# A row-maximum kernel: the last three rows in four pieces of three quarters of a row, with other sizes of loads and shares

## Chip, cores, metric

One NeuronCore of a Trainium2 chip. The metric is the device time of one execution in microseconds (us). A program on one core is timed in several runs. The profiled span is 1.8 us shorter than the time (162.3 of 164.08 us in the profiled run before).

## The reference

```python
x = np.random.randn(32, 512, 1024).astype(np.float32)
def reference(x):
    return np.max(x, axis=-1).astype(np.float32)     # 32 x 512 maxima
```

67.1 MB have to be read, and 16384 rows of 1024 numbers reduced. Each of the 128 partitions holds 128 rows.

## The kernel before

Rows come in loads of falling size into a ring of 46 row places. VectorE takes each row's maximum with a free-axis reduction. It is slightly too slow to reach the end with the loads (an estimate from the trace: at the 1.042 ns an element worked out in the prediction, the 83 rows left at 74.64 us would take it 88.6 us, to 163.2, and the last piece lands at 159.0), so some rows' first columns are shared: TensorE *turns* blocks of 128 columns (transposes them into PSUM), ScalarE copies them to SBUF, GpSimd takes the maximum over partitions, TensorE *sends back* the maxima (one transpose of a 1x128 line per block) into a small PSUM tile `fetched`. VectorE writes its own part of the same rows into one further column of that tile, and later *merges* the tile's columns into the result.

```python
BLOCKS = [
    [15, 15, 15, 14, 12, 11, 9, 8, 7, 6],        # rows a load, numbered 0 to 9
    [4, 3, 2, 2, 1, 1, 1],                       # loads 10 to 16; then two rows more
]
RING = 46
SHARED = {7: (2, 3), 9: (4, 4), 11: (3, 3), 13: (2, 3), 16: (1, 1)}   # load: (rows, blocks of 128 columns)
TENSOR = [                                       # TensorE's order: what, load, chunk
    ("turn", 7, 0), ("back", 7, 0), ("turn", 9, 0), ("turn", 9, 1),
    ("back", 9, 0), ("turn", 11, 0), ("turn", 11, 1), ("back", 9, 1),
    ...
]
MERGE = {8: (7,), 12: (9,), 15: (11,), 18: (13, 16)}   # after the work of load 8 merge load 7, ...
# ... (cut) ...
for j in range(len(loads)):
    # ... (cut: issue loads up to three ahead, then TensorE's orders that are due) ...
    if n > m:
        maximum(res[:, col:col + n - m], rows(j)[:, :n - m, :])          # own rows
    if m and parts < C:
        maximum(share(j)[:, parts, :], rows(j)[:, n - m:, parts * P:])   # own part of shared rows
    merge(j)
# the last two rows, as pieces of 689, 671 and 688 columns
piece = ring[:, at, :D - K]
nc.sync.dma_start(out=piece, in_=xb[:, S - 2, :D - K])
pair = xb[:, S - 2:, :].rearrange("p i d -> p (i d)")
nc.sync.dma_start(out=res[:, AT:AT + K + W], in_=pair[:, D - K:D + W])
nc.sync.dma_start(out=res[:, MID:], in_=pair[:, D + W:])
latest_row = maximum(res[:, AT - 1:AT], piece)
# ... (cut: the middle piece's two halves in one reduction, the merges) ...
maximum(res[:, I - 1:I], res[:, MID - 1:])
```

## Time and profile before

| | before |
|---|---|
| time, median (runs of the prediction) | 164.06 us |
| VectorE busy | 135.4 us |
| mean of the DMA over the span | 414 GB/s |
| last piece lands / last reduction ends | 159.0 / 160.0 us |
| GpSimd's last work ends | 158.3 us |

Lines of the timeline: start (us), length (us), engine, line, operation, out<-in, shapes, count.

```profile
149.72 1.01 PE L161 MATMUL fetched<-ident,top 1*128 1x1 f32 x8
...
152.42 0.17 DVE L168 TENSOR_REDUCE res<-fetched 128x4 f32<-128x20 f32 x1
```

The reader is to see a distance: the 6-row load's maxima are sent back by 150.73 (149.72 + 1.01), and VectorE merges them at 152.42. The merge has 1.7 us to spare, because it is asked for after load 12 only.

### The profile page before, as it was taken

Reading aid. Unit: us, or ns where it says so; the run is one execution under the profiler, and the core shown is the slowest. Engines: PE = TensorE matmul, PEld = TensorE weight load, DVE = VectorE, ACT = ScalarE, POOL = GpSimd, SP = SyncE. Lnnn points to the kernel's source line nnn. Section 1 sums busy time; section 2 is a strip of 40 time slices with the busy share of each in tenths; the row PEclk is TensorE's granted clock in tenths of the full one; section 3 lists DMA queues with packets and bytes.
Section 4 is the critical chain, followed back from the end, with each engine's and each line's share of the span. In section 5 each row is a group of like instructions: output and inputs, shape, how many; then the busy total and the mean of one; then the engine's idle time right before and its main releaser. Section 6 shows DMA issues by size and latency. Waiting matters only on the chain.

```text
span 162.3 us, 305 instructions
## 1 busy us (share of the span) xinstructions
PE 14.0 (9%) x76; PEld 12.0 (7%) x76; DVE 135.4 (83%) x35; ACT 6.3 (4%) x8; POOL 16.2 (10%) x11
## 2 busy tenths in 40 slices
PE   0000000000000000000000000000003010736540
PEld 0000000000000000000000000000002010725440
DVE  3000079995999779998999999999999999999994
ACT  3000000000000000000000000000001000222020
POOL 0000000000000000000000000000000500095970
DMA  7999699988999699999998998999999999999990
GB/s 242 485 485 454 273 485 485 485 379 348 485 485 485 285 410 452 452 452 388 497 472 371 433 455 355 436 436 420 509 396 445 452 395 396 440 411 423 405 379 18
DMA packets 3200, 67.18 MB, mean 414 GB/s; under 512 B 640, under 2 KB 640, under 8 KB 1408
## 3 DMA queue, kind: packets, MB, share of 16 engines
q1 hardware_dynamic: 2880, 67.11, 96.7%
q10 hardware_dynamic: 320, 0.07, 0.2%
HBM read 67.11 MB, written 0.07 MB: 414 GB/s over the span
## 4 chain that ended last, share of the span: by engine, by line
DVE 57%; DMA 36%; issue 5%; DVEq 0%
DVE res L168 52%; DMA ring<-in_x_dram 36%; DVE fetched L168 5%; DVEq L249 0%
## 5 line engine op out<-in xcount | busy, mean ns | idle before, releaser
L168 DVE TENSOR_REDUCE res<-ring 128x15 f32<-128x15360 f32 (+10 forms) x15 | 124.1, 8302 | 23.7 <-DMA ring<-in_x_dram 23.7
L143 POOL PARTITION_ALL_REDUCE top<-sb x7 | 16.0, 2330 | 141.8 <-ACT sb L141 141.8
L135 PE MATMUL ps<-ident,ring 128*128 128x128 f32 x38 | 9.3, 425 | 133.8 <-DMA ring<-in_x_dram 133.8
L135 PEld LDWEIGHTS ps<-ident,ring 128*128 128x128 f32 x38 | 7.5, 223 | 134.1 <-issue 127.8
L141 ACT COPY sb<-ps 128x768 f32<-128x768 f32 (+3 forms) x7 | 5.1, 739 | 150.2 <-PE ps L135 150.2
L168 DVE TENSOR_REDUCE fetched<-ring 128x2 f32<-128x1280 f32 (+3 forms) x5 | 8.5, 1699 | 0.0
L161 PE MATMUL fetched<-ident,top 1*128 1x1 f32 x38 | 4.8, 243 | 10.8 <-DVE fetched L168 7.3
L161 PEld LDWEIGHTS fetched<-ident,top 1*128 1x128 f32 x38 | 4.5, 213 | 12.5 <-issue 8.0
L168 DVE TENSOR_REDUCE res<-res 128x2 f32<-128x672 f32 (+1 forms) x2 | 1.7, 858 | 0.0
L141 ACT ACT_TABLE_LOAD x1 | 1.3, 1283 | 0.7 <-PEq L238 0.7
L83 DVE MEMSET ident<- 128x128 f32 x1 | 0.2, 165 | 0.8 <-PEq L238 0.8
L168 DVE TENSOR_REDUCE res<-fetched 128x2 f32<-128x8 f32 (+3 forms) x5 | 0.7, 158 | 0.0
L90 DVE TENSOR_SCALAR rowno<-rowno 32x1 f32<-32x1 f32 x3 | 0.4, 146 | 0.1
L85 DVE TENSOR_TENSOR_SCAN colno<-ident 128x128 f32<-128x128 f32 x1 | 0.4, 425 | 0.0
L92 DVE TENSOR_SCALAR ident<-colno,rowno 128x128 f32<-128x128 f32 x1 | 0.3, 285 | 0.0
L87 DVE STREAM_TRANSPOSE rowno<-colno 128x32 f32<-128x32 f32 x1 | 0.2, 213 | 0.0
L238 POOL MEMSET const-float32-0.0<- 128x1 f32 x1 | 0.1, 98 | 0.2 <-issue 0.2
L238 POOL MEMSET const-bfloat16-1.0<- 128x1 bf16 x1 | 0.1, 101 | 0.0
L238 POOL MEMSET const-uint8-127<- 128x1 uint8 x1 | 0.1, 101 | 0.0
L238 POOL MEMSET const-float32-1.0<- 128x1 f32 x1 | 0.1, 99 | 0.0
L84 DVE MEMSET rowno<- 128x32 f32 x1 | 0.1, 85 | 0.0
## 6 DMA issues: line engine op xcount, KB each, us to landing
ring<-in_x_dram SPq DMA_DIRECT2D x3, 7680.0 KB, 38.4
ring<-in_x_dram SPq DMA_DIRECT2D x1, 7168.0 KB, 37.0
ring<-in_x_dram SPq DMA_DIRECT2D x1, 6144.0 KB, 33.4
ring<-in_x_dram SPq DMA_DIRECT2D x1, 5632.0 KB, 28.6
ring<-in_x_dram SPq DMA_DIRECT2D x1, 4608.0 KB, 39.1
ring<-in_x_dram SPq DMA_DIRECT2D x1, 4096.0 KB, 33.3
ring<-in_x_dram SPq DMA_DIRECT2D x1, 3584.0 KB, 29.0
ring<-in_x_dram SPq DMA_DIRECT2D x1, 3072.0 KB, 35.9
```

The lines of the kernel that those rows point to most:

```text
L83: in_turn("DVE", nc.vector.memset(ident, 1.0))
L84: in_turn("DVE", nc.vector.memset(rowno, 0.0))
L85: in_turn("DVE", nc.vector.tensor_tensor_scan(out=colno, data0=ident, data1=ident, initial=-1.0, op0=ALU.add, op1=ALU.mult))
L87: in_turn("DVE", nc.vector.transpose(out=rowno, in_=colno[:, :32]))
L90: in_turn("DVE", nc.vector.tensor_scalar(out=part, in0=part, scalar1=float(q * 32), scalar2=None, op0=ALU.add))
L92: in_turn("DVE", nc.vector.tensor_scalar(out=ident, in0=colno, scalar1=rowno[:, 0:1], scalar2=None, op0=ALU.is_equal))
L135: in_turn("PE", nc.tensor.transpose(out=ps[:, k * P:(k + 1) * P], in_=rows(j)[:, loads[j][1] - m + r + i, c0 * P:(c0 + 1) * P], identity=i ...
L141: in_turn("ACT", nc.scalar.copy(out=sb[:, :W], in_=ps[:, :W]))
L143: in_turn("POOL", nc.gpsimd.partition_all_reduce(top[:, :W], sb[:, :W], P, bass_isa.ReduceOp.max))
L161: in_turn("PE", nc.tensor.transpose(out=share(j)[:, c0, r + i:r + i + 1], in_=tops[j, c][0:1, k * P:(k + 1) * P], identity=ident[0:1, 0:1],))
L168: return in_turn("DVE", nc.vector.reduce_max(out=out, in_=in_, axis=X))
L238: nc = _bacc.Bacc("TRN2", target_bir_lowering=False, num_devices=1)
```

## The change

Intent: the last three rows come in four pieces of three quarters of a row; VectorE takes maxima of quarters, which one more instruction merges; GpSimd ends sooner, for the latest shared row falls away. To fit, the sizes of the loads and the shares are drawn anew. The core of the diff:

```diff
-    [15, 15, 15, 14, 12, 11, 9, 8, 7, 6],
-    [4, 3, 2, 2, 1, 1, 1],
+    [15, 15, 15, 14, 11, 10, 9, 9, 8, 6],
+    [4, 3, 2, 2, 1, 1],
-SHARED = {7: (2, 3), 9: (4, 4), 11: (3, 3), 13: (2, 3), 16: (1, 1)}
+SHARED = {8: (3, 3), 9: (5, 2), 10: (3, 3), 11: (2, 3), 13: (2, 3)}
 TENSOR = [
-    ("turn", 7, 0), ("back", 7, 0), ("turn", 9, 0), ("turn", 9, 1),
-    ("back", 9, 0), ("turn", 11, 0), ("turn", 11, 1), ("back", 9, 1),
-    ("turn", 13, 0), ("back", 11, 0), ("back", 11, 1), ("turn", 16, 0),
-    ("back", 13, 0), ("back", 16, 0),
+    ("turn", 8, 0), ("turn", 8, 1), ("back", 8, 0), ("back", 8, 1),
+    ("turn", 9, 0), ("turn", 9, 1), ("turn", 10, 0), ("turn", 10, 1),
+    ("back", 9, 0), ("back", 9, 1), ("turn", 11, 0), ("back", 10, 0),
+    ("back", 10, 1), ("turn", 13, 0), ("back", 11, 0), ("back", 13, 0),
 ]
-MERGE = {8: (7,), 12: (9,), 15: (11,), 18: (13, 16)}
+MERGE = {9: (8,), 10: (9,), 12: (10,), 14: (11,), 18: (13,)}
 # ... (the three pieces of before are removed) ...
+    last = xb[:, S - 3:, :].rearrange("p i d -> p (i d)")
+    for t in range(3):
         # ... (cut: place in the ring) ...
+        nc.sync.dma_start(out=piece, in_=last[:, t * 3 * Q:(t + 1) * 3 * Q])      # Q = 256
+        inst = maximum(tail[:, 7 + 3 * t:10 + 3 * t], piece.rearrange("p (q d) -> p q d", d=Q))
         # ... (cut: the stores' dependence on the second piece) ...
+        merge(len(loads) + t)
+    nc.sync.dma_start(out=tail[:, 16:], in_=last[:, 9 * Q:])
+    maximum(res[:, I - 3:I - 1], tail[:, 7:15].rearrange("p (r q) -> p r q", q=4))
+    maximum(res[:, I - 1:], tail[:, 15:])
```

More of the change, by code (lines that the diff above doesn't have):

```diff
@@ L59 @@
     ring = once.tile([P, RING, D], F32)
-    W = 336
-    K = W - 1
-    AT = I + 16
-    MID = AT + K + W + 17
-    res = once.tile([P, MID + D - W], F32)
+    res = once.tile([P, I], F32)
+    Q = D // 4
+    tail = once.tile([P, 16 + 3 * Q], F32)
     latest = {}
@@ L98 @@
     for sizes in BLOCKS:
-        S = sum(sizes) + 2 * (sizes is BLOCKS[-1])
+        S = sum(sizes) + 3 * (sizes is BLOCKS[-1])
         xb = xf[first * P:(first + S) * P, :].rearrange("(p i) d -> p i d", p=P)
@@ L199 @@
         back(i, c)
-    if at + 1 > RING:
-        at = 0
-    piece = ring[:, at, :D - K]
-    nc.sync.dma_start(out=piece, in_=xb[:, S - 2, :D - K])
-    pair = xb[:, S - 2:, :].rearrange("p i d -> p (i d)")
-    nc.sync.dma_start(out=res[:, AT:AT + K + W], in_=pair[:, D - K:D + W])
-    nc.sync.dma_start(out=res[:, MID:], in_=pair[:, D + W:])
-    latest_row = maximum(res[:, AT - 1:AT], piece)
-    merge(len(loads))
-    maximum(
-        bass.AP(tensor=res.tensor, offset=res.offset + I - 2,
-                ap=[list(res.ap[0]), [MID - 1 - (I - 2), 2]]),
-        res[:, AT - 1:AT + K + W].rearrange("p (r k) -> p r k", r=2))
-    merge(len(loads) + 1)
-    maximum(res[:, I - 1:I], res[:, MID - 1:])
+    last = xb[:, S - 3:, :].rearrange("p i d -> p (i d)")
+    for t in range(3):
+        if at + 1 > RING:
+            at = 0
+        piece = ring[:, at, :3 * Q]
+        at += 1
+        nc.sync.dma_start(out=piece, in_=last[:, t * 3 * Q:(t + 1) * 3 * Q])
+        inst = maximum(tail[:, 7 + 3 * t:10 + 3 * t], piece.rearrange("p (q d) -> p q d", d=Q))
+        if t == 1:
+            latest_row = inst
+        merge(len(loads) + t)
+    nc.sync.dma_start(out=tail[:, 16:], in_=last[:, 9 * Q:])
+    maximum(res[:, I - 3:I - 1], tail[:, 7:15].rearrange("p (r q) -> p r q", q=4))
+    maximum(res[:, I - 1:], tail[:, 15:])
     for p, q in ((0, 48), (48, 96), (96, P)):
```

## The prediction

A wait of about 0.5 us makes 164.55 (from 164.06), no wait 164.1, weighed about 3 to 1 that is 164.45 us.

> **What bounds the kernel now.** I read the page's tenths first, then the chain of waits, then the DMA issues together with the times of issue, and last the timeline of the final 35 us.
>
> The tenths (40 slices of the span) and the DMA's busy share:
>
> ```profile
> PE   0000000000000000000000000000003010736540
> DVE  3000079995999779998999999999999999999994
> POOL 0000000000000000000000000000000500095970
> DMA  7999699988999699999998998999999999999990
> ```
>
> Two rows are full at once. The DMA is full from the first slice to the last but one; VectorE idles only in the first half and is full afterwards. GpSimd and TensorE work only in the last quarter, where they take some columns off VectorE's hands. The chain of waits says which of the two full rows ended last:
>
> ```profile
> DVE 57%; DMA 36%; issue 5%; DVEq 0%
> ```
>
> In order of time (start, us) that chain leaves the DMA at 74.6 us and never comes back to it:
>
> ```profile
> 37.60 37.02 DMA ring<-in_x_dram
> 74.62 0.02 issue
> 74.64 55.86 DVE res L168 x5
> 130.50 1.40 DVE fetched L168
> ```
>
> But VectorE is only just not waiting. Landings follow from the DMA issues (last column: us from issue to landing) plus the time of issue. The last four rows of the page's kind, and the issue times in the timeline:
>
> ```profile
> ring<-in_x_dram SPq DMA_DIRECT2D x1, 344.5 KB, 18.3
> res<-in_x_dram SPq DMA_DIRECT2D x1, 344.0 KB, 11.5
> res<-in_x_dram SPq DMA_DIRECT2D x1, 335.5 KB, 14.3
> ```
>
> ```profile
> 138.93 0.33 SPq L204 DMA_DIRECT2D ring<-in_x_dram  x1
> 143.82 0.33 SPq L206 DMA_DIRECT2D res<-in_x_dram  x1
> 147.52 0.33 SPq L207 DMA_DIRECT2D res<-in_x_dram  x1
> ```
>
> So the last three pieces land at 157.2, 158.1 and 159.0 us, and VectorE takes them up at 157.34, 158.24 and 159.15:
>
> ```profile
> 157.34 0.86 DVE L168 TENSOR_REDUCE res<-ring 128x1 f32<-128x689 f32 x1
> 158.24 0.85 DVE L168 TENSOR_REDUCE res<-res 128x2 f32<-128x672 f32 x1
> 159.01 0.22 DVE L168 TENSOR_REDUCE res<-fetched 128x2 f32<-128x8 f32 x2
> 159.15 0.86 DVE L168 TENSOR_REDUCE res<-res 128x1 f32<-128x689 f32 x1
> 160.04 0.36 ACTq L223 DMA_DIRECT2D out_dram<-res  x1
> ```
>
> The end is thus: last landing (about 159.0), 0.15 us for the last merges, one short reduction of 0.86, the last store. VectorE and the DMA reach it together, with 0.1 to 0.2 us between them. A change gains only if it brings both forward; it loses if it holds up either.
>
> [...]15 rows took 16154 ns and one row 1214, so (16154-1214)/14336 = 1.042 ns an element, and 147 ns fixed. [...]the trace shows starts about 85 ns earlier than the previous end, so I charge 62 ns fixed from start to start (147-85), and 70 to 80 ns for a merge. [...]the trace's landings (74.62, 89.13, 102.48, 113.36, 123.1, 131.6, 138.9, 143.8, 147.5) are 1.204 us a row of 524288 bytes plus 0.078 per transfer, which is 435 GB/s. [...]
>
> **The change part by part.**
>
> *Loads.* Before: 17 loads of rows and 3 pieces; after: 16 and 4. Both are 20 transfers of the same 67.11 MB. Nothing is queued late: every load of the tail is issued 9 us and more before it starts to flow, and the new ring places wait for the same or earlier reductions. So the running totals give the landings of after: the first four as before (74.62), then 11 rows 87.9, 10 rows 100.1, 9 rows 111.0, 9 rows 121.9, 8 rows 131.6, 6 rows 138.9, 4 rows 143.8, 3 rows 147.5, 2 rows 150.0, 2 rows 152.5, 1 row 153.8, 1 row 155.0. Each piece is 0.75*1.204+0.078 = 0.98 us: 156.0, 157.0, 158.0, 159.0. The last landing does not move.
>
> *VectorE's sum from 74.64 on.* Columns given to TensorE and GpSimd: 38 blocks of 128 before, 40 after; 256 elements less, -0.27 us. Reductions: 24 before, 27 after, 3*62 ns = +0.19. Net -0.08 us: nothing. The last piece has 769 elements against 689, so the last reduction is 948 ns against 861: +0.09. In front of it stand two merges as before (the last shared one, and the one that merges the quarter maxima).
>
> *VectorE without any other wait.* Starts, each 1.042 ns an element plus 62 ns: 14 rows 74.64; 11 rows 89.64; 10 rows 101.44; 9 rows 112.17; 9 rows 121.92 (landed 121.9); 5 rows 131.63; the 3x640 part 137.03, and done at 139.18 as the profile reports ends. Load of 6 rows: one row 139.09, the 5x768 part 140.23, merge 144.30. Load of 4: one row 144.37, 3x640 145.51, merge of the load of 6 wanted at 147.57. From there on the landings and the work interleave within 0.1 us, and the end comes at 160.0, against 160.01 before.
>
> *The helpers' path to that merge.* It is the part that I believe is too late. TensorE takes its work in order, and sends back the maxima of the load of 8 before it turns the load of 6. In the trace before, sending back waited for VectorE's own part of the same tile:
>
> ```profile
> PE fetched L161 <- DVE fetched L168: 7.3, 1, 7.3
> ```
>
> VectorE's part ended at 131.90 and TensorE began at 132.05, 0.15 later. After: part done 139.18, sending back 139.33, 9 blocks at 0.11 = 1.0 to 1.1, turning the load of 6 starts at 140.4 and not at 138.96. Then as in the load with 1024 columns before:
>
> ```profile
> 138.96 3.67 PE L135 MATMUL ps<-ident,ring 128*128 128x128 f32 x16 [6.15 <-DMA ring<-in_x_dram]
> 140.97 1.01 ACT L141 COPY sb<-ps 128x1024 f32<-128x1024 f32 x1 [15.38 <-PE ps L135]
> 142.07 6.43 POOL L143 PARTITION_ALL_REDUCE top<-sb  x2 [13.89 <-ACT sb L141]
> ```
>
> From turning to copy 2.0, to GpSimd 1.1, GpSimd 3.22 for 1024 columns: done at 146.7. The remaining 256 columns: GpSimd took 0.78 for 128 and 1.50 for 384, so 1.14 between; done at 147.8. Sending back 2 blocks and the signal, 0.35: 148.1 to 148.2. VectorE wants the merge at 147.57, so it stands still for 0.5 to 0.65 us.
>
> *What is left of it.* VectorE has nearly no slack afterwards, so the delay travels: from 148.2 the starts are 3 rows' first row 148.27, its part 149.41, 2 rows 150.80, merge 152.99, part 153.07, row 154.46, merge 155.60, row 155.68, pieces 156.82, 157.69, 158.56, merges 159.43, last 159.58, end 160.5. Later helpers are in time: GpSimd ends at about 157.5 against 158.28 before, and the last merge is wanted at 159.4. The end moves by +0.5, of 160.01.
>
> **The rivals.** (1) The wait in the middle is not there, because the sending back of the load of 8 does not wait for VectorE or GpSimd is quicker: then the last landing rules and the time is 164.06 to 164.15. For it: whoever chose these sizes fitted the other loads within 0.1 us. Against it: the 7.3 us wait above, of the same kind. (2) The new sizes save: GpSimd's earlier end takes the late shared work from the tail. At best the end is the last landing plus 0.03 plus 0.95, or 163.95 us in all; against it, the chain before has no GpSimd in it at all, so its earlier end buys nothing. (3) The pieces load worse or better: their lines are 3072 bytes against 2684 to 2756. Three pieces before took 2.67 us where the row rate gives 2.64, so this is within 0.05. (4) A later helper is also late, for the delayed sending back moves the whole GpSimd queue: then 164.8 to 165.
>
> **Range and chances.** A wait of 0.5 to 0.65 that travels gives 164.06+0.5 = 164.55; no wait gives 164.1. I weigh them about 3 to 1: 164.45 us, and 164.0 to 164.9 should hold it 8 times in 10. Two per cent would be 3.3 us, which no term here reaches: faster 0.01, same 0.98, slower 0.01.
>
> **What would show it.** Right: VectorE has a gap of about half a microsecond near 148 us before the merge of 5 maxima, ended by TensorE; the last four landings at 156.0 to 159.0; VectorE working without a gap from then to the end; the last reduction 948 ns. Wrong: no gap there (rival 1), a last landing moved by more than 0.2 us (loads), a gap before the merges of 3 or 2 maxima (rival 4), or the quarter reductions costing well over 0.95 us each.

## The result

The changed kernel took 164.70 us (median of 6 runs, 164.53 to 164.79) against 164.06 (163.92 to 164.10): a ratio of 1.004, 95% interval 1.0027 to 1.0053. Ratios here are the mean time of one kernel's fast runs over that of the other's in the same rounds, so not quite the ratio of the two medians. It is slower by about 0.6 us, clear of the noise and far within 2%.

The changed kernel's tenths:

```profile
PE   0000000000000000000000000000000050757730
...
DVE  3000079995999689998999999999999999998994
...
POOL 0000000000000000000000000000000009079960
DMA  7998899988999699999989979999999999999980
```

The helpers start two slices later (slice 32 and not 30), and VectorE, full before up to the last slice, shows an 8 in the fourth slice from the right (146.5 to 150.6 us). The chain of waits now has the helpers in it:

```profile
DMA 55%; DVE 36%; PE 3%; POOL 2%; issue 2%; ACT 1%; DVEq 1%; ACTq 0%
```

The DMA's larger share (36% before) is no part of the loss. VectorE takes up load 7 as it lands, after 0.04 us idle, so here the chain goes back through the DMA; in a second profile of the same kernel (e8, told below), where that idle is 0.02 us, it goes through VectorE and the DMA has 35.4%.

The same chain in order of time (start, us, what), from the end of VectorE's work on load 8 to the merge of load 9's five maxima:

```profile
137.01 2.08 DVE fetched L165
139.09 0.14 issue
139.23 1.08 PE fetched L158 x9
140.31 1.92 PE ps L132 x8
...
142.31 1.02 ACT sb L138
...
143.41 3.23 POOL top L140
...
146.69 1.01 PE fetched L158 x8
...
147.74 0.38 PE fetched L158 x2
...
148.14 1.30 DVE res L165 x2
```

Loads are numbered from 0: in the changed kernel load 8 has 8 rows, load 9 has 6, load 10 has 4 and load 11 has 3. This is one loop through four engines. TensorE sends back load 8 (`fetched`) 0.14 us after VectorE's part of load 8 is written, then turns load 9 (`ps`), ScalarE copies, GpSimd reduces, TensorE sends back load 9 in two chunks, VectorE merges at 148.14. In the view of waits, the two lines that belong to it (total us, times, longest us):

```profile
PE fetched L158 <- DVE fetched L165: 5.5, 1, 5.5
...
DVE res L165 <- PE fetched L158: 0.6, 1, 0.6
```

Of these only the second costs: the idle of TensorE would be free, were it not in front of the loop (the like wait before, 7.3 us, held up nothing: VectorE waited for no TensorE there). And the timeline, with the idle before an instruction in brackets:

```profile
148.14 0.17 DVE L165 TENSOR_REDUCE res<-fetched 128x5 f32<-128x15 f32 x1 [0.61 <-PE fetched L158]
...
156.74 2.66 DVE L165 TENSOR_REDUCE tail<-ring 128x3 f32<-128x768 f32 x3
...
159.31 0.16 DVE L165 TENSOR_REDUCE res<-fetched 128x2 f32<-128x8 f32 x1
159.43 1.02 DVE L165 TENSOR_REDUCE res<-tail 128x2 f32<-128x8 f32 x2
160.49 0.36 ACTq L217 DMA_DIRECT2D out_dram<-res  x1
```

VectorE stands still for 0.61 us before the merge and not once after it. The last reduction ends at 160.46 where it ended at 160.01, although its piece, issued at 147.42 and 11.4 us on the way, lands at 158.8, if anything a little sooner than the 159.0 of before:

```profile
tail<-in_x_dram SPq DMA_DIRECT2D x1, 384.0 KB, 11.4
```

So VectorE, which took the last piece up 0.15 us after the landing before, is 0.7 us behind it now. The loads are cleared. (In this profile all landings are 0.14 us earlier from the very first load on, 21.25 and not 21.39. A second profile of the changed kernel, told below, had its last landing at 158.97 and its last reduction at 160.62: 0.6 us behind the 160.01 of before at like landings.) GpSimd does end sooner, at 157.5 and not 158.3:

```profile
155.03 2.50 POOL L140 PARTITION_ALL_REDUCE top<-sb  x1 [0.76 <-ACT sb L138]
```

### The profile page after: what moved, and what is told of

Read it like the earlier page. It is cut to its first block, busy times and chain, and to the rows that moved or that the text cites. A ratio compares the mean times of both kernels' runs of the same rounds, so it can differ in the third digit from the quotient of the medians.

```text
span 162.8 us, 320 instructions
## 1 busy us (share of the span) xinstructions
PE 15.0 (9%) x80; PEld 12.6 (8%) x80; DVE 135.3 (83%) x38; ACT 6.6 (4%) x9; POOL 17.3 (11%) x12
## 3 DMA queue, kind: packets, MB, share of 16 engines
q1 hardware_dynamic: 2880, 67.11, 96.5%
HBM read 67.11 MB, written 0.07 MB: 413 GB/s over the span
## 4 chain that ended last, share of the span: by engine, by line
DMA 55%; DVE 36%; PE 3%; POOL 2%; issue 2%; ACT 1%; DVEq 1%; ACTq 0%
DMA ring<-in_x_dram 55%; DVE res L165 32%; POOL top L140 2%; DVE fetched L165 2%; PE fetched L158 2%; DVE tail L165 1%; PE ps L132 1%; ACT sb L138 1%; DVEq L243 1%; ACTq L138 0%
## 5 line engine op out<-in xcount | busy, mean ns | idle before, releaser
L165 DVE TENSOR_REDUCE res<-ring 128x1 f32<-128x1024 f32 (+7 forms) x15 | 119.2, 7969 | 23.6 <-DMA ring<-in_x_dram 23.5
L140 POOL PARTITION_ALL_REDUCE top<-sb x8 | 17.1, 2181 | 140.0 <-ACT sb L138 139.8
L132 PE MATMUL ps<-ident,ring 128*128 128x128 f32 x40 | 9.8, 426 | 133.0 <-DMA ring<-in_x_dram 133.0
L165 DVE TENSOR_REDUCE fetched<-ring 128x3 f32<-128x1920 f32 (+2 forms) x5 | 11.4, 2283 | 0.0
L158 PE MATMUL fetched<-ident,top 1*128 1x1 f32 x40 | 5.3, 243 | 10.4 <-DVE fetched L165 5.5
L165 DVE TENSOR_REDUCE tail<-ring 128x3 f32<-128x768 f32 x3 | 2.7, 945 | 0.0
L165 DVE TENSOR_REDUCE res<-fetched 128x3 f32<-128x12 f32 (+2 forms) x5 | 0.8, 161 | 0.6 <-PE fetched L158 0.6
L165 DVE TENSOR_REDUCE res<-tail 128x2 f32<-128x8 f32 (+1 forms) x2 | 1.0, 552 | 0.0
```

Source lines behind the costliest of these rows:

```text
L132: in_turn("PE", nc.tensor.transpose(out=ps[:, k * P:(k + 1) * P], in_=rows(j)[:, loads[j][1] - m + r + i, c0 * P:(c0 + 1) * P], identity=i ...
L140: in_turn("POOL", nc.gpsimd.partition_all_reduce(top[:, :W], sb[:, :W], P, bass_isa.ReduceOp.max))
L158: in_turn("PE", nc.tensor.transpose(out=share(j)[:, c0, r + i:r + i + 1], in_=tops[j, c][0:1, k * P:(k + 1) * P], identity=ident[0:1, 0:1],))
L165: return in_turn("DVE", nc.vector.reduce_max(out=out, in_=in_, axis=X))
```

## The experiments

Theory A: the loop is late at the merge of load 9, VectorE waits 0.61 us there, and has no slack behind it. Rivals: B, the new pieces, the extra merge and the longer last reduction cost the time; C, the helpers are late everywhere; D, GpSimd's work is too long whatever TensorE's order. Each kernel was timed in 5 rounds; "before" in the same rounds was 164.03 to 164.06.

| label | what | median us | ratio to before, 95% | wait at the merge of load 9, us |
|---|---|---|---|---|
| e8_changed_again | the change | 164.59 | 1.0034 (1.0022 to 1.0047) | 0.62 |
| e1_merge_later | merge one load later | 164.23 | 1.0005 (0.9993 to 1.0018) | none |
| e2_turn_first | TensorE's order | 164.02 | 0.9993 (0.9981 to 1.0006) | none |
| e3_part_first | VectorE's order | 164.05 | 0.9997 (0.9984 to 1.0009) | none |
| e4_sizes_only | new sizes, old tail | 164.63 | 1.0031 (1.0017 to 1.0045) | 0.61 |
| e5_pieces_only | old sizes, new tail | 164.04 | 1.0000 (0.9988 to 1.0013) | none |
| e6_longer_wait | later sending back | 166.75 | 1.0164 (1.0150 to 1.0178) | 2.73 |
| e7_sizes_turn_first | e4 with e2's order | 164.18 | 1.0008 (0.9996 to 1.0021) | none |
| e9_changed_less_work | the change, less work behind the wait | 164.22 | 1.0011 (0.9999 to 1.0024) | 0.61 |
| e10_no_wait_less_work | e2, the same work less | 164.11 | 1.0007 (0.9993 to 1.0020) | none |

### Which part of the change: e4 and e5

The two halves of the change, each alone. e4 puts the tail of before behind the new sizes (a seventh load in the second block, of one row, then the old three pieces; the lines are against the changed kernel):

```diff
-    [4, 3, 2, 2, 1, 1],
+    [4, 3, 2, 2, 1, 1, 1],
-    (the four pieces of three quarters of a row)
+    (the three pieces of before)
```

> The new sizes of loads and shares with the tail of the kernel before (one more 1-row load, then three pieces of two rows). Theory A: the wait of 0.6 us near 147.5 us is there, and only the shorter last reduction (861 ns for 942) comes back: 164.5 to 164.7 us, ratio 1.003 to 1.004. Theory B (the new pieces cost the time): back to 164.1, ratio 1.000 to 1.001.

e5 puts the new tail behind the old sizes (the lines are against the kernel before):

```diff
-    [4, 3, 2, 2, 1, 1, 1],
+    [4, 3, 2, 2, 1, 1],
-SHARED = {7: (2, 3), 9: (4, 4), 11: (3, 3), 13: (2, 3), 16: (1, 1)}
+SHARED = {7: (2, 3), 9: (4, 4), 11: (3, 3), 13: (2, 3)}
 # ... (cut: TENSOR and MERGE lose load 16) ...
-    (three pieces of two rows)
+    (four pieces of three rows)
```

> The kernel before with the new tail alone: the last 1-row load (and its shared block of 128 columns) and the three pieces of two rows become four pieces of three quarters of a row; all other sizes and shares as before. Theory A (the new tail is neutral): no gap on VectorE over 0.1 us from 75 us on, end within 0.1 us of before, 164.0 to 164.15, ratio 0.9995 to 1.001, although GpSimd ends about 0.7 us earlier. Theory B (the tail costs the time): 164.4 or more. The intent of the change (GpSimd ending sooner shortens the end) would show as 163.8 or less.

Measured: 164.63 with the sizes alone, 164.04 with the pieces alone. The whole loss comes with the sizes and shares; B falls. e4 has the same wait in the view of waits:

```profile
DVE res L165 <- PE fetched L158: 0.6, 1, 0.6
```

e4's expectation also counted on 0.08 us coming back from the shorter last reduction. That can't be seen: e4 lies 0.59 us above before, the changed kernel 0.53 in its own second measurement, and from the row after the merge of load 11 to the end of the last reduction e4 takes 4.91 us (155.64 to 160.55), the changed kernel 4.85 (155.61 to 160.46). The section on e7 has the likely reason: the old tail's second reduction starts late, and does so in e4 too (35 ns of idle before it, at 158.79).

In e5 the granted TensorE clock was 0.947 in the profiled run and not 1.0. TensorE is not on its chain. That run, 164.16, was the slowest of the five, 0.12 us above their median; another run at 0.947 took just that median, 164.04. The tail of e5's timeline:

```profile
156.30 2.69 DVE L167 TENSOR_REDUCE tail<-ring 128x3 f32<-128x768 f32 x3
158.91 0.16 DVE L167 TENSOR_REDUCE res<-fetched 128x2 f32<-128x8 f32 x1
159.03 1.02 DVE L167 TENSOR_REDUCE res<-tail 128x2 f32<-128x8 f32 x2
```

It ends at 160.05, before at 160.01. The new tail is worth nothing either way (164.04 us against 164.06), though GpSimd ends at 157.6 there and not at 158.3: VectorE waits for loads (23.7 us in four waits) and for no helper in e5, so GpSimd ends 0.7 us sooner without any gain, and the intent of the change fails on this.

### Taking the wait away in three ways: e1, e2, e3

e1 leaves the loop late and asks for its result later:

```diff
-MERGE = {9: (8,), 10: (9,), 12: (10,), 14: (11,), 18: (13,)}
+MERGE = {9: (8,), 11: (9,), 12: (10,), 14: (11,), 18: (13,)}
```

> The changed kernel with one number different: the five maxima of the load of 6 rows are merged one load later (after the 3-row load's work, not after the 4-row load's). Theory A (the 0.61 us wait before that merge is the whole loss): no gap before this merge, VectorE takes it up near 150.8 us, end 0.5 to 0.6 us earlier than in the changed kernel, 164.05 to 164.2 us, ratio to the kernel before 1.000 to 1.001. Theory B (pieces, extra merges and the longer last reduction cost the time, the wait only uses up slack): the gap goes but the time stays above 164.4, ratio 1.003 or more. Theory C (the helpers are late everywhere): the wait comes back before the next merge, of the 4-row load's maxima.

The wait is gone and the time 164.23, just over A's upper 164.2, with a ratio inside A's. B's 164.4 is not reached. Of C something is true: before the merge of load 10 VectorE now idles 0.04 us, and before that of load 11 0.12 us, since TensorE ends sending back load 11 at 155.07 and VectorE's work before the merge ends at 154.98. Asking later cures one merge, and the late loop shows up, smaller, at the next ones.

e2 changes TensorE's order alone:

```diff
-    ("turn", 8, 0), ("turn", 8, 1), ("back", 8, 0), ("back", 8, 1),
-    ("turn", 9, 0), ("turn", 9, 1), ("turn", 10, 0), ("turn", 10, 1),
+    ("turn", 8, 0), ("turn", 8, 1), ("turn", 9, 0), ("turn", 9, 1),
+    ("back", 8, 0), ("back", 8, 1), ("turn", 10, 0), ("turn", 10, 1),
```

> The changed kernel with TensorE's order alone different: it turns the load of 6 rows before it sends back the maxima of the load of 8, so the turning no longer stands behind the wait for VectorE's part of that tile. Theory A (TensorE's order makes GpSimd start 1.3 us late): turning starts at 138.9 and not 140.25, the copy at about 140.9, GpSimd at 142.1, the sending back of the load of 6 then waits only for the turning of the next load (done at 146.0) and ends near 147.3; the gap on VectorE shrinks from 0.61 to under 0.1, time 164.05 to 164.2. Theory D (GpSimd's work on 1024 and 256 columns is too long whatever the order): the gap stays 0.4 us or more and the time above 164.45.

TensorE's timeline in e2:

```profile
138.94 2.37 PE L132 MATMUL ps<-ident,ring 128*128 128x128 f32 x10 [5.20 <-DMA ring<-in_x_dram]
141.23 1.11 PE L158 MATMUL fetched<-ident,top 1*128 1x1 f32 x9
```

Load 9 is turned the moment it lands (138.94 and not 140.25), its maxima are back at 147.14, and VectorE merges at 147.43 without a gap. The time is 164.02, 0.57 us below the changed kernel's second measurement and level with before. D falls: GpSimd's two reductions take the same 3.22 and 1.14 us in both kernels, and they are only begun 1.2 us sooner.

e3 leaves TensorE's order and changes VectorE's, so that what TensorE waits for is ready sooner:

```diff
+        if m and parts < C:
+            maximum(share(j)[:, parts, :], rows(j)[:, n - m:, parts * P:])
         if n > m:
             maximum(res[:, col:col + n - m], rows(j)[:, :n - m, :])
-        if m and parts < C:
-            maximum(share(j)[:, parts, :], rows(j)[:, n - m:, parts * P:])
```

> The changed kernel with VectorE's order alone different: in each shared load VectorE reduces its part of the shared rows first and its own rows after. Theory A (sending back the load of 8 waits for the end of VectorE's part, at 139.08 us): that part ends at about 133.7, sending back starts when GpSimd is done, near 138.0, the turning of the load of 6 starts at 139.0, and the gap before the merge of five goes from 0.61 to under 0.1; time 164.05 to 164.2. If instead sending back waited for something else of VectorE, the turning stays at 140.2 and the time at 164.6 to 164.8.

TensorE in e3:

```profile
136.59 0.79 PE L158 MATMUL fetched<-ident,top 1*128 1x1 f32 x6 [2.85 <-POOL top L140]
137.99 0.47 PE L158 MATMUL fetched<-ident,top 1*128 1x1 f32 x3 [0.61 <-POOL top L140]
138.94 2.37 PE L132 MATMUL ps<-ident,ring 128*128 128x128 f32 x10 [0.47 <-DMA ring<-in_x_dram]
```

Now sending back waits for GpSimd alone, is over before load 9 lands, and the time is 164.05. This is the plainest test of the first link: the same instructions on the same engines (their order is changed in all five shared loads), and moving VectorE's part of load 8 forward by 5.4 us sets TensorE free. The columns that TensorE writes and the column that VectorE writes are different ones of the same PSUM tile, and still TensorE was idle for 5.48 us in the changed kernel until VectorE's write was done. That sharing one tile is the reason is argued, not shown: no run split them into two tiles.

### Making the wait longer: e6

```diff
-    ("back", 9, 0), ("back", 9, 1), ("turn", 11, 0), ("back", 10, 0),
+    ("turn", 11, 0), ("back", 9, 0), ("back", 9, 1), ("back", 10, 0),
```

> The changed kernel with the wait made longer on purpose: TensorE turns the 3-row load (landing at 147.4) before it sends back the maxima of the load of 6, which can then be merged near 150.15 us and not 148.14. Theory A (VectorE has no slack after that merge, so the end follows the wait one to one): wait 2.6 to 2.7 us instead of 0.61, time 2.0 to 2.1 us above the changed kernel, 166.7 to 166.8, no other gap. If there were slack behind the merge, the time rises by under 1.5 us.

```profile
DVE res L165 <- PE fetched L158: 2.7, 1, 2.7
```

Wait 2.73 and not 0.62, time 166.75 and not 164.59: 2.11 us more wait, 2.16 us more time. One to one: there is no slack behind the merge.

### Less work behind the wait: e9 and e10

Both reduce only half of each row in loads 12 and 14, so 1.6 us of VectorE's work is missing (the comparison with the reference passed it all the same, so it would not have told; the trace shows the shorter shapes). Their outputs are wrong, which doesn't matter for the times. e9 does this to the changed kernel, e10 to e2:

```diff
+            cut = H if j in (12, 14) else D
-            maximum(res[:, col:col + n - m], rows(j)[:, :n - m, :])
+            maximum(res[:, col:col + n - m], rows(j)[:, :n - m, :cut])
```

> Wrong result on purpose: the changed kernel, where VectorE reduces only half of each row of the 2-row load (the first of them) and of the 1-row load after the second, 1.6 us less work behind the wait. Theory A (the wait costs what it does because VectorE has no slack behind it): the gap of 0.61 us before the merge of five stays, but VectorE catches up before the pieces, with new small gaps (the next merges are wanted sooner than TensorE has sent them, up to about 0.16 us late at the merge of the 3-row load); time 164.05 to 164.2. If the wait cost time in some other way than through VectorE's work, the time stays at 164.5 or more.

> Wrong result on purpose: the same cut of 1.6 us of VectorE's work in the kernel where TensorE turns the load of 6 first (no wait, 164.02 us). If the landings bind the end beside VectorE, as the prediction had it, nothing comes back: VectorE waits for the loads instead, gaps of over 1 us in sum ended by the DMA or by merges, last landing and last reduction where they were, 163.95 to 164.1. If VectorE alone binds, the time falls towards 162.5.

e9 keeps the wait of 0.61 us and still comes back to 164.22 (a hair above the expected 164.2): with slack behind it, most of the wait costs nothing. What it keeps are two new waits for TensorE, 0.39 and 0.65 us, at the next two merges; in e10, with the early loop, the same two are 0.33 and 0.31 us, so the rest is the late loop again. e10 stays at 164.11. VectorE's timeline there:

```profile
151.65 0.17 DVE L165 TENSOR_REDUCE res<-fetched 128x3 f32<-128x12 f32 x1 [0.33 <-PE fetched L158]
152.46 1.49 DVE L165 TENSOR_REDUCE fetched<-ring 128x2 f32<-128x1280 f32 x1 [0.64 <-DMA ring<-in_x_dram]
153.87 0.68 DVE L165 TENSOR_REDUCE res<-ring 128x1 f32<-128x512 f32 x1
154.85 0.17 DVE L165 TENSOR_REDUCE res<-fetched 128x2 f32<-128x8 f32 x1 [0.31 <-PE fetched L158]
```

The 1.6 us turn into idle, for the next load or the next merge: 0.33, 0.64 and 0.31 us, and each start after a wait also loses the 85 ns or so by which starts without a wait come before the end of the work before them (150.10 and 150.19 here): an estimate of 1.28 + 3 x 0.085 = 1.5. Two of the three waits are for TensorE, so not every step is held by a landing; but the last reduction starts at 159.05, 0.16 us after the last landing (158.89), against 0.17 before (159.15 and 158.98). Without the wait, the landings hold the end where it is, and a VectorE with less to do gains nothing. That is the bound of e2 and, by the same 0.17 us, of the kernel before, shown from the other side.

### A version to beat both: e7, and the control e8

> The new sizes with TensorE turning the load of 6 before sending back the load of 8, and the tail of the kernel before (last reduction 689 elements, one merge in front of it and not two). Theory A: no gap, the last reduction starts 0.1 us after the last landing and takes 0.86, so up to 0.1 us under the kernel with the new pieces and the same order of TensorE: 163.9 to 164.05, ratio 0.9985 to 1.0005. It can't gain more, for the last landing does not move.

e7 is e4 with e2's order of TensorE, and was to gain up to 0.1 us from the shorter last reduction. It missed: 164.18. The last reduction is indeed shorter (0.87 us), but it starts only at 159.18. VectorE takes up the last one-row load as it lands (156.26 us), now with all of its 1024 columns (896 in the kernel before), and then has no pause left: from the first piece's start to the middle one's it takes 0.90 us, not the 0.78 of 689 columns, for the old tail's middle reduction starts 35 ns after the first one's end (158.25 to 158.29), where others start some 85 ns before it. That it reads the first one's maximum is the likely reason: in the kernel before the same pair has 158.20 and 158.24, and in the changed kernel the reduction that reads the quarter maxima starts 30 ns after the end of the last of them (159.40 and 159.43). The expectation had left both out. No version tried is faster than before beyond the noise; e2, e3 and e5 equal it.

> The changed kernel itself, on the same chip and in the same rounds as the three others: 164.6 to 164.75 us, ratio 1.003 to 1.0045, with the gap of 0.61 us before the merge of five.

The control agrees with the first measurement within 0.11 us: 164.59 us, just under the expected 164.6, and a wait of 0.62 us.

## Why the prediction was right

- **Loads.** Right. Last landing predicted at 159.0, seen at 158.8 and 158.97. One clause was off: it said that the new ring places wait for the same or earlier reductions, but load 10 was issued only after the 10-row load's reduction, at 112.1 and not at 103.5 as before. The load before it landed at 138.8 and load 10 at 143.7, 4.9 us later, as the rate of the landings before gives for its four rows (4 x 1.204 + 0.078 = 4.89), so this cost nothing.
- **VectorE's sum.** Right. 135.3 us busy against 135.4. The quarter reductions took 945 ns, the last 942, with 948 predicted.
- **The helpers' path.** Right, link by link: VectorE's part done 139.08 (said 139.18), sending back 139.23 (139.33), turning 140.25 (140.4), GpSimd done 146.64 and 147.68 (146.7 and 147.8), merge at 148.14 (148.1 to 148.2), wait 0.61 (0.5 to 0.65). The largest miss in it is the last link: from GpSimd's end to the merge 0.46 us passed, where 0.35 was said. e2 and e3 cut the path in two places, and each removes the loss.
- **What is left of it.** Right in kind: no gap after the merge, the last reduction ending at 160.46 (160.5). e6 shows one to one. The size was a little low: a shift of 0.5 was said, the medians differ by 0.64 in the first measurement and 0.53 in the second. The 160.46 fits so well partly by luck: this profile's landings are 0.14 us early. At the landings of before it would be about 160.60 (an estimate from these numbers; the second profile has 160.62), 0.59 after 160.01 and thus the whole wait of 0.61, not its lower end of 0.5.
- **The stated time.** 164.45 was said, 164.70 measured. The difference is the weight of one in four given to rival 1 (0.1 us of it) and the size of the shift. Rival 1 was the wrong one: the earlier wait of 7.3 us, of the same kind and harmless in the kernel before, was the telling line. Rival 2 is refuted by e5 (its best case was mis-added, too: 0.98 after 159.0 is 0.03 before the 160.01 of before, so 164.03 and not 163.95), rival 3 by e5's last landing (158.96, and 158.98 before). Rival 4 did not happen in the changed kernel, but its small form did in e1 and e9.

## What to carry to other kernels

Where several engines form a loop, look not only at who waited, but at what stood behind the waiter in its queue. Here TensorE waited 5.48 us for VectorE's part of load 8; the like wait in the kernel before, 7.30 us, was harmless, but in the changed kernel the turning of load 9 stood behind it and began at 140.25 us and not at 138.94 (e2). Such a wait cost only what VectorE could not catch up later: 2.11 us more of it cost 2.16 us (e6), and with 1.6 us less work behind it the same 0.61 us left the time at 164.22 and not at 164.59 (e9, e8). So test a wait by making it longer and by taking away work behind it. And GpSimd's earlier end, 157.6 and not 158.3, was worth nothing in e5 (164.04 us against 164.06), where VectorE waited for no helper.

## What the traces measured

- Loads: with this one core running the program, 67.11 MB came at 414 GB/s over the whole span of the kernel before, and at 433 GB/s within it (the load of 14 rows, 7.34 MB in the 16.95 us between its landing, 74.62, and the one before, 57.67).
- A further load on the queue costs 0.08 us here (worked out in the prediction from the landings: 0.078 beside 1.204 a row).
- The partition all-reduce of GpSimd over 128 partitions took 0.78 us for 128 columns, 1.50 for 384, 2.50 for 768 and 3.22 for 1024 in the kernel before (a second one of 1024 columns 3.30), and 1.14 for 256 in the changed kernel.
